# Group B's outputs summed by parts: the running product meets the steps of v

## The chip, the cores and the metric

The kernel runs on one core of a Trainium2 chip. The metric is the time of one execution on the device in microseconds (us), taken as the median of several runs. Matmuls and transposes run on TensorE (PE), elementwise work on VectorE (DVE), ScalarE (ACT) and GpSimd (POOL). The queue of SyncE (SP) issues most transfers (DMAs), which 16 DMA engines carry out. SBUF is the on-chip memory with 128 partitions, PSUM the one that matmuls write.

## The reference

One layer of a hybrid encoder over 1024 frames of width 1024: a normalisation, one projection to q, k and v, eight heads of chunked softmax attention (group A), eight heads of stick-breaking attention (group B), an output projection with a residual, and a gated channel mixer with a short convolution. The change concerns group B. Cut to what matters:

```python
for blk in range(S // Q_BLOCK):                 # 128 queries each
    z = einsum('bqhd,bkhd->bhqk', qb, kb) * scale
    causal = s_idx < t_idx                      # key strictly before query
    log_beta = log_sigmoid(z)
    log_1m = where(causal, log_beta - z, 0.0)   # log(1 - sigmoid(z))
    suffix = cumsum(log_1m, reverse=True) - log_1m
    a = where(causal, exp(log_beta + suffix), 0.0)
    outs.append(einsum('bhqk,bkhd->bqhd', a, vb))
```

The weight of a key is the sigmoid of its score times the product of (1 - sigmoid) over all keys between it and the query. With r(s) for the product of (1 - sigmoid) over the keys from s to the query, the weight of key s is r(s+1) - r(s).

## The kernel before

The program goes through stages: a start (the v projection, then q and k of the first head pair), group B, group A, the output projection, and the channel mixer. Keys and queries of group B are stored in reversed order of frames, so that the sum over earlier keys is a scan to the right. Two heads make a pair n (0 to 3); q, k and v of a pair fill 128 partitions or 128 columns.

**An item of group B** is one head h of one block i of 128 queries (class BlockB). ORDER_B runs the blocks 7, 0, 6, 1, 5, 2, 4, 3; block i has 8 - i key blocks, so its width is w = (8 - i) x 128 columns, 128 for block 7 and 1024 for block 0. PE computes the scores z into a PSUM tile (L803 and L804, names zb_i_h; the tiles come from a ring of two with the tag "big"), ACT makes them 1 - sigmoid (L812), DVE turns that into the running product by one scan (L813, into one of three acts tiles of 1025 columns, whose first column is 0), and a subtraction of neighbours over the full width gives the weights (L820). Two items later PE transposes the weights in blocks of 128 keys (L839, names tpb_i_h), ACT copies them to SBUF (L843, tb), and PE multiplies them with v to the outputs (L853, names yb). DVE copies these to y (L1214); once a pair is done they are split in two parts (yb again, L1153 and L1162) and stored to memory (spill, L1159).

**The filler.** Between these PE steps stand matmuls of the next pair's q and k projections (L145, into q_p and k_p), so that PE has work while an item waits for ACT and DVE. RATE_B says how many microseconds of them a group of 16 items gets. A projected half goes through DVE (L641, q_f and k_f), ACT and DVE again (L123), and POOL and a few transfers on SP bring its rows in place (L650, L663).

**The order of the work.** PE's order is written out. That of DVE, ACT, POOL and of SP's transfers is set by a planner (class Flow): chains of operations with estimated durations, of which always the one that can start first is emitted. Every engine runs its own list in order: an operation that waits holds up all behind it. The planner's clock goes by PE's estimated work and knows a transfer by a fixed rate and latency.

**v** was written to memory (v_d) by the v projection, 128 rows by (8 key blocks, 4 pairs, 128 columns) for each group. load_v(n) (L771) brings v of a pair to a tile v of 128 partitions (keys of a block) by 8 x 128, in one transfer, with four such buffers. Before group B it is called for n = 0 to 3, then for n + 4 after the last outputs of pair n. At the start q0 and k0 are projected in two halves of 512 frames, both halves in one PSUM tile of two banks.

Of the kernel before, what the change touches and what calls it, by code (L numbers as in the profile page):

```python
# [9 lines left out]
F32 = mybir.dt.float32  # L10
# [6 lines left out]
P = 128  # L17
# [3 lines left out]
G = 2  # L21
# [39 lines left out]
def tile_hybrid_block(  # L61
# [45 lines left out]
        return pool.tile(list(shape), dt, tag=tag, name=name)  # L107

    cst = one("cst", "cst", shape=(P, C_N))
    nc.scalar.dma_start(cst, consts)  # L110

    def c1(off):
        return cst[:, off : off + 1]
# [76 lines left out]
    with tc.tile_pool(name="kp", bufs=2) as kp:  # L190
# [280 lines left out]
        class Chain:  # L471


            def __init__(self, ops, t, after, behind, slack):
                self.ops, self.t, self.behind, self.slack = list(ops), t, behind, slack
                self.after = [a for a in after if a]
                self.begun = self.done = False

        class Flow:
# [14 lines left out]
            def start(self, c):  # L494
                if c.behind and not c.behind.begun or not all(a.done for a in c.after):
                    return None
                return max([c.t] + [self.free[e] for e in c.ops[0][0]] + [a.t for a in c.after])

            def step(self, limit=float("inf")):
                best = None  # L500
                for c in self.chains:
                    t = self.start(c)
                    if t is not None and t <= limit and (best is None or t < best[0]):
                        best = t, c
                if best is None:
                    return False
                t, c = best
# [38 lines left out]
        def on_s(n, do):  # L546
            return "S", n / 1200 + 0.1, 0.1, do
# [4 lines left out]
        def load(kb, do, us=2.2):  # L552
            return "D", kb / 260, us, do

        class Ring:
# [5 lines left out]
            def chain(self, *ops, after=(), then=(), slack=SLACK):  # L561

                head = flow.add(ops[0], after=[self.users[0], *after], behind=self.last)
                rest = flow.add(*ops[1:], after=[head, *then], slack=slack)
                self.users.popleft()
                self.users.append(rest)
                self.last = head
                return head, rest
# [40 lines left out]
        def fetch(queue=w_ready, pool=wp, tags=("wh", "wl"), bufs=None):  # L609

            if not w_next:
                return
            if (w_next[0] in LATE_W) != (queue is w_late):
                w_missed.append(1)
                return
            name, t, loaded = w_next
            w_next.clear()

            def high():
                t["h"] = pool.tile([P, D], F32R, tag=tags[0], name=f"{name}_h", bufs=bufs)  # L620
# [7 lines left out]
            c = flow.add(on_s(D, high), rest, after=[loaded], slack=SLACK)  # L628
            queue.append((t, c))
            load_next([c])  # L630

# [133 lines left out]

        def load_v(n):

            v_of[n] = kp.tile([P, T], F32, tag="v", name=f"v{n}", bufs=4)
            src = v_d[n // 4].rearrange("p (t n c) -> p t n c", n=4, c=P)[:, :, n % 4, :]
            v_chains[n] = [  # L770
                flow.add(load(512, lambda: nc.sync.dma_start(  # L771
                    v_of[n].rearrange("p (t c) -> p t c", c=P), src
                ), 4.0))
            ]

        HS = (A, B)

        class BlockB:

# [11 lines left out]
            def scores(self, h):  # L791
                i, nk = self.i, self.nk
                qa, qb, ka, kb, la, lb = qk_of[self.n]
                q, k, l = ((qa, ka, la), (qb, kb, lb))[h]
                z, mine = bigs.get(f"z{self.nm}_{h}")
                w = nk * P

                at, parts = {
                    1: (P, ((0, 2 * P, -P),)), 5: (192, ((192, 320, 0), (GW, 320, 320))),
                }.get(nk, (0, ((0, GW, 0), (GW, w - GW, GW)) if nk > 4 else ((0, w, 0),)))  # L800
                for o, n, k0 in parts:
                    ks = slice(i * P + k0, i * P + k0 + n)
                    PE.matmul(z[:, o : o + n], q[:, cols(i)], k[:, ks], start=True, stop=False)  # L803
                    PE.matmul(z[:, o : o + n], q[:, cols(i)], l[:, ks], start=False, stop=True)  # L804
# [6 lines left out]
                self.chain[h] = flow.add(  # L811
                    on_s(w + 75, lambda: S.activation(z, z, AF.Sigmoid, scale=-1.0)),  # L812
                    on_v(2 * w + 70, lambda: V.tensor_tensor_scan(  # L813
                        out=a[:, 1 : w + 1], data0=z, data1=first[:, :w], initial=1.0, op0=ALU.mult,
                        op1=ALU.max,
                    )),
                )
                mine.append(self.chain[h])
                self.chain[h] = flow.add(
                    on_v(w, lambda: V.tensor_tensor(  # L820
                        out=a[:, 1:w], in0=a[:, 1:w], in1=a[:, 2 : w + 1], op=ALU.subtract
                    ), "VL"),
                    after=[self.chain[h]],
                )
# [21 lines left out]
            def output(self, yy):  # L846
                ready(*self.turned)
                i, nk = self.i, self.nk
                v = v_of[self.n]
                for j in range(nk):  # L850
                    for h in range(2):
                        off = (i + j) * P + h * 64
                        PE.matmul(  # L853
                            yy[HS[h], :], v[:, off : off + 64],
                            self.at[h][:, self.c0[h] + j * P : self.c0[h] + (j + 1) * P],
                            start=j == 0, stop=j == nk - 1, skip_group_check=True,
                        )
                flow.work(0.218 * nk + 0.15)
# [209 lines left out]
        flow.free.update(V=START, S=START)  # L1068
        qk_chains[0] = []
        for what, stack in (("q", stack_q), ("k", stack_k)):  # L1070
            o = big(f"{what}0_p")
            outs = [o[:, rows(g)] for g in range(G)]
            st = stack(0, outs)
            w = pre["qk".index(what)]
            for g in range(G):
# [6 lines left out]
                qk_chains[0].append(next(st)[1])  # L1082
            fetch()
        S.preload_act_table_set("sigmoid_and_others")
        for n in range(4):
            load_v(n)
        flow.drain()
        start.__exit__(None, None, None)
# [82 lines left out]
            spilled[n] = flow.add(*ops, after=sum(parts, []) + spilled[n - 1 : n], slack=SLACK)  # L1171

        with stage("b"):
            b_acts = [pools["sbuf"].tile([P, T + 1], F32, tag=f"b{i}", name=f"acts{i}", bufs=1) for i in range(3)]
            for t in b_acts:
                GP.memset(t[:, :1], 0.0)
# [10 lines left out]
            for b in range(len(items) + 3):  # L1187
# [15 lines left out]
                if ending:  # L1203
# [82 lines left out]
        for b in range(len(blocks) + 2):  # L1286
# [13 lines left out]
            if b in (2, 3):  # L1300
                g = b - 2
                rn_chains["b", g] = flow_totals(yb_of[0][:, rows(g)], f"nb_{g}", rn2[:, 4 * g : 4 * g + 4])
                if g == 1:
                    rn_chains["b"] = flow_root(rn2, [rn_chains["b", g] for g in range(G)])
            if cur and cur.i == 2:
                if cur.p < 3:
                    load_bias(cur.p + 1)
# [779 lines left out]
def _layout(inputs):  # L2087
# [8 lines left out]
    def tiles(w):  # L2096
# [12 lines left out]
            cols(a("norm1_g")[0]), cols(a("norm2_g")[0]), cols(a("norm_a_g")[0]),  # L2109
            cols(a("norm_b_g")[0]), cols(a("final_g")), cols(conv_w[0]), cols(conv_w[1]),  # L2110
            cols(conv_w[2]), cols(a("conv_b")[0]), np.broadcast_to(rel[:, -1], (P, 8)),
        ],
        axis=1,
    )
# [32 lines left out]
```

## Time and profile before

| | us |
|---|---|
| median of 3 runs | 1218.7 (1218.18 to 1219.36) |
| the profiled execution | 1219.38 |
| its span in the trace | 1217.6 |
| PE busy in it | 1200.3 |
| DVE busy | 947.7 |
| ACT busy | 670.4 |
| POOL busy | 163.8 |

The span is what the hardware profiler saw between the first and the last instruction; the execution's own time has 1.8 us around it. An engine's busy time is the time in which it executes. Rows of groups give line, engine, operation, output and inputs, shape and count; then the busy time of all, the mean of one in ns, the idle time ahead of them, and what ended it. Rows of the timeline begin with start and duration in us; a bracket at their end gives the idle time ahead and its releaser. Group B runs from about 111 to 330 us, the start before it, group A after it.

### The profile page before, as it was taken

The numbers are of one execution on the slowest core, as the hardware profiler recorded it, in microseconds if no ns is written. First come the engines' busy times: TensorE is split into PE (matmuls) and PEld (weight loads), VectorE is DVE, ScalarE is ACT, GpSimd is POOL, SyncE is SP. The second block draws the span as 40 slices with busy tenths as digits, with TensorE's granted clock in tenths as the row PEclk, the third lists the DMA queues.
The fourth block names the chain that finished last, engine by engine and source line by source line (L and its number), as shares of the span: only waits on it lengthen the run. The fifth ranks groups of instructions, "written<-read, shape, count | busy, mean of one in ns | idle before, by whom it ended". The sixth has DMA issues, their size and how long they took to land.

```text
span 1217.6 us, 17209 instructions
## 1 busy us (share of the span) xinstructions
PE 1200.3 (99%) x6476; PEld 995.5 (82%) x6476; DVE 947.7 (78%) x1417; ACT 670.4 (55%) x1180; POOL 163.8 (13%) x128
## 2 busy tenths in 40 slices
PE   9999999999999999999999999999999999999997
PEld 6787888888878888888878888888888888888887
DVE  7945878889567677559997768777687779969896
ACT  7863454554576766434575555545555455444424
POOL 0002101212211112133000000000000023042036
PEclk9999999999999999999999999999999999999999
DMA  8354323433523382134032132221222196420003
GB/s 297 95 195 135 99 82 87 113 110 93 143 72 93 77 265 72 68 112 149 16 122 93 64 104 72 84 91 65 104 72 85 56 368 268 174 103 1 1 1 139
DMA packets 60323, 135.19 MB, mean 111 GB/s; under 512 B 6736, under 2 KB 18128, under 8 KB 60240
## 3 DMA queue, kind: packets, MB, share of 16 engines
q1 hardware_dynamic: 60096, 133.98, 33.7%
q8 instruction: 51, 0.84, 0.3%
q14 instruction: 32, 0.26, 0.1%
q10 hardware_dynamic: 144, 0.11, 0.1%
HBM read 89.24 MB, written 28.31 MB: 97 GB/s over the span
## 4 chain that ended last, share of the span: by engine, by line
PE 82%; DVE 7%; DMA 4%; ACT 3%; issue 2%; POOL 1%; SPq 0%; DVEq 0%; ACTq 0%; POOLq 0%
PE u_a L1563 9%; PE u_c L1563 9%; PE u_e L1563 8%; PE dz L2062 8%; PE q_p L145 6%; PE k_p L145 6%; PE u_b L1563 4%; PE dj L2062 4%; PE dm L2062 4%; PE v_x L454 3%; PE pa L145 3%; PE tpb L839 3%; PE yb L853 3%; PE v_y L454 2%; PE pb L145 2%
## 5 line engine op out<-in xcount | busy, mean ns | idle before, releaser
L813 DVE TENSOR_TENSOR_SCAN acts<-zb,first 128x128 f32<-128x128 f32 (+7 forms) x64 | 86.1, 1351 | 22.3 <-ACT zb L812 22.0
L843 ACT COPY tb<-tpb 128x128 f32<-128x128 f32 (+3 forms) x96 | 43.4, 483 | 62.3 <-PE tpb L839 61.6
L1587 DVE SCALAR_TENSOR_TENSOR vt<-cv,cst,vt 128x1023 f32<-128x1023 f32 (+1 forms) x44 | 58.2, 1322 | 2.2 <-ACT vt L1581 1.4
L1587 DVE SCALAR_TENSOR_TENSOR gt<-cg,cst,gt 128x1023 f32<-128x1023 f32 (+1 forms) x44 | 56.5, 1285 | 1.6 <-ACT gt L1581 0.8
L123 POOL TENSOR_TENSOR dx_0wl<-dr,dx_0wh 128x512 fp32r<-128x512 f32 x1 | 1.4, 1371 | 412.3 <-ACT dx_0wh L1829 412.3
L934 ACT ACTIVATE pa<-sa,sta 128x640 f32<-128x640 f32 (+4 forms) x64 | 42.3, 661 | 23.4 <-DVE sta L920 18.6
L812 ACT ACTIVATE zb<-zb 128x128 f32<-128x128 f32 (+7 forms) x64 | 41.2, 644 | 17.9 <-PE zb L804 17.1
L959 ACT COPY pta<-tpa 128x512 f32<-128x512 f32 (+3 forms) x80 | 37.2, 476 | 22.7 <-PE tpa L955 22.4
L145 PE MATMUL q_p<-hTh,q_h 128*128 128x512 f32 x112 | 47.4, 423 | 0.0
L820 DVE TENSOR_TENSOR acts<-acts 128x127 f32<-128x127 f32 (+7 forms) x64 | 46.8, 750 | 0.7
L1581 ACT ACTIVATE gt<-cg,cst 128x1024 f32<-128x1024 f32 x22 | 27.4, 1245 | 36.0 <-DVE cg L1455 35.9
L145 PE MATMUL k_p<-hTh,k_h 128*128 128x512 f32 x112 | 46.3, 413 | 0.4 <-DVE q_f L641 0.4
L145 PE MATMUL q_p<-hTh,q_l 128*128 128x512 f32 x112 | 44.1, 394 | 0.0
L145 PE MATMUL k_p<-hTl,k_h 128*128 128x512 f32 x112 | 44.0, 393 | 0.0
L123 POOL TENSOR_TENSOR q_l<-q_r,q_h 128x1024 fp32r<-128x1024 f32 x7 | 16.9, 2419 | 201.2 <-ACT q_h L621 146.8
L145 PE MATMUL k_p<-hTh,k_l 128*128 128x512 f32 x112 | 44.0, 393 | 0.0
L145 PE MATMUL q_p<-hTl,q_h 128*128 128x512 f32 x112 | 44.0, 392 | 0.0
L839 PE MATMUL tpb<-ident,acts 128*128 128x128 f32 x288 | 42.8, 276 | 0.2
L920 DVE TENSOR_REDUCE sta<-sa 128x1 f32<-128x640 f32 (+4 forms) x64 | 41.9, 655 | 1.3
L839 PEld LDWEIGHTS tpb<-ident,acts 128*128 128x128 f32 x288 | 33.8, 140 | 9.9 <-ACT tb L843 2.1
L1452 DVE TENSOR_TENSOR up_r<-up_r 128x512 f32<-128x512 f32 x60 | 41.2, 687 | 0.8
L955 PE MATMUL tpa<-ident,pa 128*128 128x128 f32 x240 | 38.7, 278 | 1.9 <-ACT pta L959 0.9
(1313 smaller groups left out, 3916.3 us busy)
## 6 DMA issues: line engine op xcount, KB each, us to landing
up_r<-in_w_up_dram SPq DMA_DIRECT2D x44, 512.0 KB, 3.6
act<-vt SPq DMA_DIRECT2D x22, 512.0 KB, 2.6
dr<-in_w_dn_dram SPq DMA_DIRECT2D x20, 512.0 KB, 6.8
dr<-act SPq DMA_DIRECT2D x20, 512.0 KB, 7.5
wv<-in_w_v_dram SPq DMA_DIRECT2D x16, 256.0 KB, 5.4
xin<-in_xT_dram SPq DMA_DIRECT2D x16, 256.0 KB, 5.4
row<-in_x_rows_dram SPq DMA_DIRECT2D x16, 256.0 KB, 2.6
v<-v_d SPq DMA_DIRECT2D x8, 512.0 KB, 5.3
```

What stands on the lines that cost most here:

```text
L145: PE.matmul(o, w[:, sl], t[:, rows(g)], start=first and i == 0, stop=last and i == 2,)
L454: PE.matmul(bank[j], t[:, cols(j)], w, start=p in (1, 5) and k == 0 and i == 0, stop=k == 3 and i == 2, skip_group_check=True,)
L812: on_s(w + 75, lambda: S.activation(z, z, AF.Sigmoid, scale=-1.0)),
L813: on_v(2 * w + 70, lambda: V.tensor_tensor_scan(out=a[:, 1 : w + 1], data0=z, data1=first[:, :w], initial=1.0, op0=ALU.mult, op1=ALU.max,)),
L820: on_v(w, lambda: V.tensor_tensor(out=a[:, 1:w], in0=a[:, 1:w], in1=a[:, 2 : w + 1], op=ALU.subtract), "VL"),
L839: PE.transpose(tp[:, cols(b)], self.a[h][:, cols(b0 + b)], ident)
L843: mine.append(flow.add(on_s(m * P, lambda o=o, tp=tp: S.copy(o, tp))))
L920: V.tensor_reduce(out=st[:, 0:1], in_=full, axis=AX.XY if nk == 5 else AX.X, op=ALU.max, negate=True,)
L934: on_s(w + 170, lambda: S.activation(po, full, AF.Exp, bias=st[:, 0:1], accum_out=st[:, 1:2])),
L1563: PE.matmul(o, w[:, cols(k)], t, start=start and k == 0 and i == 0, stop=k == 3 and i == 2, skip_group_check=True,)
L1587: V.scalar_tensor_tensor(out=t[:, : T - lag], in0=o[:, lag:], scalar=c1(c + ct), in1=t[:, : T - lag], op0=ALU.mult, op1=ALU.add,)
L2062: PE.matmul(o[m], w[:, cols(m)], t, start=i in (0, 1, 4, 5) and p == ps_[0] and j == 0, stop=p == ps_[-1] and j == 2, skip_group_check=True,)
```

## The change

The sum over keys of (r(s+1) - r(s)) v(s) is rearranged: it is the sum of r(s) times a step of v between neighbouring keys, with the ends kept apart. So the scan's result is transposed as it is, and a second array dv, v's neighbour minus v, takes the place of v in the outputs. For the first 128 keys of a block's list, which hold the diagonal, weights are still made, by a subtraction over 127 columns, and meet v.

The parts:

- the subtraction after the scan covers 127 columns for every item; the acts tiles have 1024 columns and need no memset;
- load_v brings for a pair of group B a tile dv and a tile v by four transfers (128 rows; 127 rows, shifted by one; the last row from the other blocks, 7 x 128; 128 zeros from widened constants), and DVE subtracts one from the other (128x1024, in place);
- with two tiles for each pair in the same four buffers, pairs 0 and 1 are loaded ahead of group B, pair 2 after pair 0, pair 3 after pair 1, pairs 4 and 5 after pair 2, pairs 6 and 7 in group A;
- the halves of q0 and k0 get PSUM tiles of their own, q's with the tag "big", k's with "pj";
- RATE_B is 19 for 20;
- the planner breaks ties: among chains that can start at the same time it takes the one that was ready first, with 1 us added for the weights' chains and those of the rings.

```diff
-RATE_B, LEAD_B = 20.0, 8.0
+RATE_B, LEAD_B = 19.0, 8.0
+DUE = 1.0
...
-                return max([c.t] + [self.free[e] for e in c.ops[0][0]] + [a.t for a in c.after])
+                ready = max([c.t] + [a.t for a in c.after])
+                return max([ready] + [self.free[e] for e in c.ops[0][0]]), ready + c.due
...
-            v_of[n] = kp.tile([P, T], F32, tag="v", name=f"v{n}", bufs=4)
             src = v_d[n // 4].rearrange("p (t n c) -> p t n c", n=4, c=P)[:, :, n % 4, :]
-            v_chains[n] = [
-                flow.add(load(512, lambda: nc.sync.dma_start(
-                    v_of[n].rearrange("p (t c) -> p t c", c=P), src
-                ), 4.0))
-            ]
...
+            d, o = whole(f"dv{n}")
+            v, nxt = whole(f"v{n}")
+            v_of[n] = v, d
+
+            def bring():
+                nc.sync.dma_start(o, src)
+                nc.sync.dma_start(nxt[: P - 1], src[1:])
+                nc.sync.dma_start(nxt[P - 1 :, : KT - 1, :], src[:1, 1:, :])
+                nc.sync.dma_start(nxt[P - 1 :, KT - 1, :], consts[:1, C_N:])
+
+            v_chains[n] = [flow.add(
+                load(1024, bring, 5.0),
+                on_v(T, lambda: V.tensor_tensor(out=d, in0=v, in1=d, op=ALU.subtract), "VL"),
+            )]
...
-                        out=a[:, 1 : w + 1], data0=z, data1=first[:, :w], initial=1.0, op0=ALU.mult,
+                        out=a[:, :w], data0=z, data1=first[:, :w], initial=1.0, op0=ALU.mult,
...
-                    on_v(w, lambda: V.tensor_tensor(
-                        out=a[:, 1:w], in0=a[:, 1:w], in1=a[:, 2 : w + 1], op=ALU.subtract
+                    on_v(P, lambda: V.tensor_tensor(
+                        out=a[:, : P - 1], in0=a[:, : P - 1], in1=a[:, 1:P], op=ALU.subtract
...
-                            yy[HS[h], :], v[:, off : off + 64],
+                            yy[HS[h], :], (d if j else v)[:, off : off + 64],
...
-            o = big(f"{what}0_p")
-            outs = [o[:, rows(g)] for g in range(G)]
+            outs = [(big if what == "q" else pj)(f"{what}0_p{g}")[:, :GW] for g in range(G)]
...
-        for n in range(4):
+        for n in range(2):
             load_v(n)
...
-                        load_v(n + 4)
+                        for m in ((2,), (3,), (4, 5), ())[n]:
+                            load_v(m)
```

In the two programs an instruction's line differs (L771 before is L791 to L794 after, L820 is L847, L813 is L840, L641 is L646, L123 is L124, L803 and L804 are L830 and L831, L839 is L866, L145 is L146). A number at a name's end only tells one tile from the next.

SP's list at the end of the start, before, from the last raw weights of pair 0 (k_r and q_r are raw weights of the next pair; v_949 to v_952 are v of pairs 0 to 3; qb and qa are pieces of the next pair's q):

```order
L605 DMA k_r<-in_w_in_dram 128x1024
L771 DMA v_949<-v_d_111 128x8x128
L771 DMA v_950<-v_d_111 128x8x128
L771 DMA v_951<-v_d_111 128x8x128
L605 DMA q_r<-in_w_in_dram 128x1024
L771 DMA v_952<-v_d_111 128x8x128
```

And after (dv_951 and v_952 belong to pair 0, dv_953 and v_954 to pair 1):

```order
L609 DMA k_r<-in_w_in_dram 128x1024
L791 DMA dv_951<-v_d_111 128x8x128
L792 DMA v_952<-v_d_111 127x8x128
L793 DMA v_952<-v_d_111 1x7x128
L794 DMA v_952<-in_consts_dram 1x128
L791 DMA dv_953<-v_d_111 128x8x128
L792 DMA v_954<-v_d_111 127x8x128
L793 DMA v_954<-v_d_111 1x7x128
L794 DMA v_954<-in_consts_dram 1x128
L609 DMA q_r<-in_w_in_dram 128x1024
```

Four transfers of 128 rows became two of 128 rows, two of 127 rows and four of one row, all behind the same k_r.

DVE's list at the start of group B, before, from the last operation on k0:

```order
L123 TENSOR_TENSOR lb_914<-k_f_955,kb_912 64x512
L641 SCALAR_TENSOR_TENSOR q_f_1045<-q_p_1008,rb_802 128x512
L123 TENSOR_TENSOR q_f_1045<-q_f_1045,qa_1033 128x512
L813 SCALAR_TENSOR_TENSOR acts_998<-zb_7_0_1052,first 128x128
L820 TENSOR_TENSOR acts_998<-acts_998 128x127
L641 SCALAR_TENSOR_TENSOR q_f_1076<-q_p_1035,rb_802 128x512
L813 SCALAR_TENSOR_TENSOR acts_999<-zb_0_0_1072,first 128x1024
```

And after:

```order
L124 TENSOR_TENSOR lb_916<-k_f_960,kb_914 64x512
L798 TENSOR_TENSOR dv_951<-v_952,dv_951 128x1024
L798 TENSOR_TENSOR dv_953<-v_954,dv_953 128x1024
L646 SCALAR_TENSOR_TENSOR q_f_1078<-q_p_1013,rb_802 128x512
L840 SCALAR_TENSOR_TENSOR acts_1006<-zb_7_0_1054,first 128x128
L646 SCALAR_TENSOR_TENSOR q_f_1087<-q_p_1040,rb_802 128x512
L840 SCALAR_TENSOR_TENSOR acts_1007<-zb_0_0_1070,first 128x1024
```

Both subtractions that make dv stand between the last operation on k0 and the first scan (a scan prints as SCALAR_TENSOR_TENSOR here, and as TENSOR_TENSOR_SCAN in the trace). On PE the scores of the third item, zb_0_1, follow those of the second directly in the changed order:

```order
L831 MATMUL zb_0_0_1070<-la_915,qa_843 128x512
L830 MATMUL zb_0_0_1070<-ka_913,qa_843 128x512
L831 MATMUL zb_0_0_1070<-la_915,qa_843 128x512
L830 MATMUL zb_0_1_1083<-kb_914,qb_844 128x512
L831 MATMUL zb_0_1_1083<-lb_916,qb_844 128x512
```

Before, 12 projection matmuls of k stood between them.

DVE's list where pair 1 begins and pair 2's v is brought, before (yb_1 is a part of pair 0's outputs, k_f a projected half of k):

```order
L813 SCALAR_TENSOR_TENSOR acts_998<-zb_1_0_1651,first 128x896
L1153 SCALAR_TENSOR_TENSOR yb_1_512_1696<-y_1051,cst,yb_0_512_1693 128x512
L641 SCALAR_TENSOR_TENSOR k_f_1701<-k_p_1532,rb_802 128x512
L820 TENSOR_TENSOR acts_998<-acts_998 128x895
L813 SCALAR_TENSOR_TENSOR acts_999<-zb_1_1_1661,first 128x896
```

And after:

```order
L840 SCALAR_TENSOR_TENSOR acts_1006<-zb_1_0_1633,first 128x896
L1179 SCALAR_TENSOR_TENSOR yb_1_512_1678<-y_1053,cst,yb_0_512_1599 128x512
L798 TENSOR_TENSOR dv_1556<-v_1557,dv_1556 128x1024
L646 SCALAR_TENSOR_TENSOR q_f_1685<-q_p_1472,rb_802 128x512
L840 SCALAR_TENSOR_TENSOR acts_1007<-zb_1_1_1646,first 128x896
L847 TENSOR_TENSOR acts_1006<-acts_1006 128x127
```

The subtraction for pair 2 stands ahead of the 127 columns of zb_1_0 (acts_1006). On PE, 36 projection matmuls stand between pair 0's last outputs and the first transposition of zb_1_0, where 45 stood; at the next change of pairs 30, where 39 stood; the subtraction for pair 3 stands there in the same way.

More of the change, by code (lines that the diff above doesn't have):

```diff
@@ L502, in step @@
                     t = self.start(c)
-                    if t is not None and t <= limit and (best is None or t < best[0]):
+                    if t is not None and t[0] <= limit and (best is None or t < best[0]):
                         best = t, c
@@ L564, in chain @@
                 rest = flow.add(*ops[1:], after=[head, *then], slack=slack)
+                head.due = rest.due = DUE
                 self.users.popleft()
@@ L628, in fetch @@
             c = flow.add(on_s(D, high), rest, after=[loaded], slack=SLACK)
+            c.due = DUE
             queue.append((t, c))
@@ L766, in load_v, with whole @@
         def load_v(n):
-            v_of[n] = kp.tile([P, T], F32, tag="v", name=f"v{n}", bufs=4)
             src = v_d[n // 4].rearrange("p (t n c) -> p t n c", n=4, c=P)[:, :, n % 4, :]
-            v_chains[n] = [
-                flow.add(load(512, lambda: nc.sync.dma_start(
-                    v_of[n].rearrange("p (t c) -> p t c", c=P), src
-                ), 4.0))
-            ]
+            def whole(name):
+                t = kp.tile([P, T], F32, tag="v", name=name, bufs=4)
+                return t, t.rearrange("p (t c) -> p t c", c=P)
+            if n >= 4:
+                v_of[n], o = whole(f"v{n}")
+                v_chains[n] = [flow.add(load(512, lambda: nc.sync.dma_start(o, src), 4.0))]
+                return
+            d, o = whole(f"dv{n}")
[10 more added lines that the diff above has]
+            )]
         HS = (A, B)
@@ L1173, in tile_hybrid_block @@
         with stage("b"):
-            b_acts = [pools["sbuf"].tile([P, T + 1], F32, tag=f"b{i}", name=f"acts{i}", bufs=1) for i in range(3)]
-            for t in b_acts:
-                GP.memset(t[:, :1], 0.0)
+            b_acts = [pools["sbuf"].tile([P, T], F32, tag=f"b{i}", name=f"acts{i}", bufs=1) for i in range(3)]
             first = pools["sbuf"].tile([P, T], BF16, tag="first", name="first", bufs=1)
```

10 lines of the change are left out of this document (7 added, 3 removed).

## The prediction

> **What bounds the kernel now.** First the busy times of the page, then the table by stage, because an average hides stages.
> ```profile
> PE 1200.3 (99%) x6476; PEld 995.5 (82%) x6476; DVE 947.7 (78%) x1417; ACT 670.4 (55%) x1180; POOL 163.8 (13%) x128
> ```
> ```profile
> core 0: us, PE busy (x) PEld busy (x) DVE busy (x) ACT busy (x) POOL busy (x), PEclk, DMA share, GB/s
> 86.00:130.00 44.00, 42.37 (x195) 34.42 (x194) 24.29 (x26) 20.16 (x31) 9.20 (x9) 1.00 0.53 160
> 130.00:180.00 50.00, 49.99 (x376) 42.01 (x374) 41.37 (x50) 25.37 (x49) 5.91 (x4) 1.00 0.32 85
> 180.00:230.00 50.00, 49.91 (x384) 41.61 (x384) 42.38 (x49) 27.90 (x53) 7.20 (x4) 1.00 0.40 110
> 230.00:280.00 50.00, 49.66 (x383) 41.55 (x379) 45.31 (x50) 27.42 (x52) 10.30 (x6) 1.00 0.40 107
> 280.00:335.00 55.00, 54.89 (x370) 46.43 (x369) 37.93 (x61) 28.17 (x52) 13.41 (x11) 1.00 0.42 113
> ```
> TensorE (PE) is busy for 1200.3 of 1217.6 us at the full granted clock. From 130 to 335 us, group B's stage, its idle time is 0.01 + 0.09 + 0.34 + 0.11 = 0.55 us. VectorE (DVE) works 41 to 45 us of each 50 there and PE never waits for it. So whatever the change saves on DVE can return at most 0.55 us; what it can cost is whatever makes PE wait. The execution took 1219.4 us, the span and 1.8 around it, and lies 0.7 above the median of the runs, 1218.7. I count from 1219.4.
>
> **The subtraction, cut to 127 columns.** It is the change's saving on DVE.
> ```profile
> L820 DVE TENSOR_TENSOR acts<-acts 128x127 f32<-128x127 f32 (+7 forms) x64 | 46.8, 750 | 0.7
> ```
> ```profile
> L820 DVE TENSOR_TENSOR acts<-acts 128x1023 f32<-128x1023 f32 x8 | 9.6, 1210 | 0.0
> L813 DVE TENSOR_TENSOR_SCAN acts<-zb,first 128x896 f32<-128x896 f32 x8 | 16.1, 2017 | 3.4 <-ACT zb L812 3.3
> L641 DVE SCALAR_TENSOR_TENSOR q_f<-q_p,rb 128x512 f32<-128x512 f32 x10 | 6.8, 679 | 3.0 <-PE q_p L145 2.9
> L813 DVE TENSOR_TENSOR_SCAN acts<-zb,first 128x128 f32<-128x128 f32 x8 | 3.3, 414 | 0.7 <-ACT zb L812 0.7
> L820 DVE TENSOR_TENSOR acts<-acts 128x127 f32<-128x127 f32 x8 | 2.3, 286 | 0.1
> ```
> 64 of them take 46.8 us; at 0.286 each 18.3 remain, and 28.5 go. The four new subtractions for dv (128x1024, the size of the 1.21 row) add 4.8. DVE loses 23.7 us, all of it beside PE's work: I take **-0.5** from the 0.55 of idle time.
>
> **PSUM tiles of q0 and k0.** The two long waits of window 86 to 130 are these.
> ```profile
> 94.58 0.39 PE L145 MATMUL q_p<-hTh,qk_l 128*128 128x512 f32 x1
> 95.81 0.50 PE L145 MATMUL q_p<-hTh,qk_h 128*128 128x512 f32 x1 [0.85 <-DVE q_f L641]
> ...
> 104.56 0.39 PE L145 MATMUL k_p<-hTh,qk_l 128*128 128x512 f32 x1
> 105.73 0.50 PE L145 MATMUL k_p<-hTh,qk_h 128*128 128x512 f32 x1 [0.78 <-DVE k_f L641]
> ```
> The second half's first matmul stands in the same PSUM tile as the first half and waits until DVE has read it. Starts lie 1.23 and 1.17 us apart where neighbours lie 0.23 apart. With a tile for each half both waits go: 1.00 + 0.94, **-1.9**. Next late is the weights' arrival, which no row shows late here.
>
> **The new load of v.** It decides the time. Before, v is one transfer of 128 rows for each pair; now a pair of group B needs two large ones and two small ones, and one large one has 127 rows (v shifted by a key). A subtraction on DVE waits for all four, and what stands behind it on DVE waits too.
> ```profile
> DMA packets 60323, 135.19 MB, mean 111 GB/s; under 512 B 6736, under 2 KB 18128, under 8 KB 60240
> ...
> v<-v_d SPq DMA_DIRECT2D x8, 512.0 KB, 5.3
> ```
> ```profile
> 102.20 0.33 SPq L605 DMA_DIRECT2D k_r<-in_w_in_dram  x1
> 102.64 3.64 SPq L771 DMA_DIRECT2D v<-v_d  x3
> ```
> ```profile
> DMA packets 2448, 1.24 MB, mean 309 GB/s; under 512 B 32, under 2 KB 2448, under 8 KB 2448
> ...
> q1 hardware_dynamic: 2448, 1.24, 112.2%
> ```
> The first row's 6736 packets under 512 B are 421 x 16, and the program issues 421 transfers: read as one closing packet from each engine, every transfer of before is cut into 16 equal shares (its row counts are 128 or 64). 127 is prime: no count from 2 to 16 divides it. So I bound the load from both sides. Spread over all engines it costs what the 512 KB row says, 5.3 us to landing. On one engine it moves 127 x 8 runs of 512 B = 520 KB at a sixteenth of the full queues' rate in the last fence (106 to 110 us), 309 / 16 = 19.3 GB/s: **27 us**. I take 27, since every transfer seen has equal shares and this one can have none.
>
> The Trainium skill, DMA: Bandwidth & Descriptors, section "Why a DMA increments its semaphore by 16 and not by 1", gives the count of engines as the largest number up to 16 that divides the slowest dimension on both sides, and names 127 partitions as a case of one engine; no run here shows such a transfer yet. By it the sum is the 1308.2 below; by an even spread it would be the 1218.0 of the first rival.
>
> *Start of group B.* In the changed order SP issues dv and v of pairs 0 and 1 behind k_r, from 102.6 us on. On the shared engine shares of 512 KB take 32.8 KB / 19.3 = 1.7 us: k_r 1.7, dv 1.7, v 27, dv 1.7, v 27, together 59; with about 2 us from issue to the first byte and landing, the last lands at 164.7. Both subtractions stand on DVE behind k0's last operation and ahead of this:
> ```profile
> 110.84 0.69 DVE L641 SCALAR_TENSOR_TENSOR k_f<-k_p,rb 128x512 f32<-128x512 f32 x1 [1.64 <-PE k_p L145]
> ...
> 116.16 0.68 DVE L123 TENSOR_TENSOR lb<-k_f,kb 64x512 fp32r<-64x512 f32 x1
> 116.87 0.69 DVE L641 SCALAR_TENSOR_TENSOR q_f<-q_p,rb 128x512 f32<-128x512 f32 x1
> ...
> 119.60 0.43 DVE L813 TENSOR_TENSOR_SCAN acts<-zb,first 128x128 f32<-128x128 f32 x1 [0.65 <-ACT zb L812]
> ```
> ```profile
> 118.80 0.28 PE L803 MATMUL zb<-ka,qa 128*128 128x256 f32 x1
> ...
> 122.46 0.39 PE L804 MATMUL zb<-la,qa 128*128 128x512 f32 x1
> 122.69 0.39 PE L145 MATMUL k_p<-hTh,k_h 128*128 128x512 f32 x1
> ```
> Last landing 164.7 + 1.2 + q_f 0.68 + scan 0.43 = 167.1, and only this scan frees the PSUM tile of zb_7_0. Two such tiles exist: zb_7_0 and zb_0_0 hold them, and zb_0_1, next on PE in the new order, needs the first. PE gets there at 122.69 - 1.9 = 120.7. **+46.4**.
>
> *Pairs 2 and 3.* v of pair 2 is asked for once pair 0's last outputs (36 matmuls from 170.98) are done, that of pair 3 once pair 1's are (from 217.41).
> ```profile
> 170.98 2.19 PE L853 MATMUL yb<-tb,v 128*64 128x128 f32 x36
> ...
> 190.59 0.27 PE L839 MATMUL tpb<-ident,acts 128*128 128x128 f32 x1
> ```
> ```profile
> 217.41 2.19 PE L853 MATMUL yb<-tb,v 128*64 128x128 f32 x36
> ...
> 235.73 0.49 PE L839 MATMUL tpb<-ident,acts 128*128 128x128 f32 x3
> ```
> Issue to landing is 0.8 + 1.7 + 27 + 2.2 = 31.7. On DVE the subtraction (1.2), q_f (0.68), a scan (2.02) and zb_1_0's 127 columns (0.29) follow before PE can transpose zb_1_0: 35.9. PE's work from the outputs' end, 172.9, to that transposition is 17.7 us with 45 projection matmuls; the lower RATE_B makes them come earlier, and in the new order 36 stand there: 9 x 0.23 less, so 15.7. **+20.2**. For pair 3 only the subtraction and one of 0.29 follow: 33.2, against 235.73 - 219.5 = 16.2 less 2.1 again (30 projection matmuls instead of 39), so 14.1. **+19.1**. Transfers queued behind these loads come later too, and PE has no more work to give them; a spill that a DVE step needs may add 3.
>
> *Restarts.* PE's first matmuls after it stood still:
> ```profile
> L212 PE MATMUL v_y<-zero x10: 379/622/634, 1.5 to 4.9; 128*128 128x512 bf16 x10
> ```
> Nine starts take 3.4 us, 0.38 each where 0.23 is normal: 1.5 us lost for ten. Three restarts: **+4.5** (0 to 6).
>
> The Trainium skill, TensorE: Matmul & The Clock Gate, Part 1, has PE at half rate after an idle window of about 3.4 us; its figure gives an estimate of 1.7 for each restart, and the L212 row agrees in kind.
>
> **RATE_B and DUE.** With projections moved earlier within each pair, those left between k of pair 3 and its first scores are 33, 33 x 0.23 = 7.5 us; from k_f at 110.84 to the first scores at 118.80 the chain took 8.0 in the trace. I take **+1** (0 to 2). The smaller memsets, the sliced constants and the new ties move nothing that PE waits for: 0.
>
> **Sum:** 1219.4 - 0.5 - 1.9 + 46.4 + 20.2 + 19.1 + 4.5 + 1 = **1308.2**.
>
> **The rivals.** *The load spreads.* If 127 rows go over many engines, the two pairs' dv and v are 2 x (0.524 + 0.520) = 2.09 MB; with k_r's 0.52 MB ahead, 2.61 MB at 309 GB/s from 102.6 us take 8.5, and with 2 us for issue and landing v of pair 1 is there at 113.1, ahead of DVE's last k0 step, which ends at 116.84 - 1.9 = 114.9 us. That landing is the point from which it decides: earlier, nothing waits and the sum is 1219.4 - 0.5 - 1.9 + 1 = 1218.0, not slower. For it speaks that the queues have room (a busy share of 0.32 to 0.42 in group B); against it, that equal shares can't be made. I give it 0.14.
> *One engine for each load, but not the same one.* Then the two first loads run side by side and end 28.7 us (v and dv) earlier: 1308.2 - 28.7 = 1279.5. No row here shows which engine a short transfer takes; 0.06.
> *A faster lone engine.* The page's busiest slice of 40 moved
> ```profile
> GB/s 297 95 195 135 99 82 87 113 110 93 143 72 93 77 265 72 68 112 149 16 122 93 64 104 72 84 91 65 104 72 85 56 368 268 174 103 1 1 1 139
> ```
> 368 GB/s, 23 for an engine: 22.6 us instead of 27, four times 4.4 less, 1308 - 17.6 = 1290. This lies inside the forecast.
>
> **How the numbers follow.** One engine 0.80 at 1308 (own range 1286 to 1328: the faster engine and no restarts below, 6 us of queued spills, restarts and three longer landings of 3 above), two engines 0.06 at 1279.5, spread 0.14 at 1218 (1216 to 1222). 8 in 10 need the first and most of the second: 1275 to 1328. A measurement of this kernel tells 0.2%, 2.4 us, from no change. Slower: 0.80 + 0.06 = 0.86; the spread case gives 0.08 to the same and 0.06 to faster.
>
> **What would show it.** Right: v's 127-row transfer takes 20 to 30 us to land, L798 waits for it on DVE, PE has one idle stretch of 40 to 50 us near 121 us and two of about 20, and q0/k0 show no wait at their second halves. Wrong: L798 starts within 2 us of the operation ahead of it, or a 127-row transfer lands like one of 128; then no term from 46.4 to 4.5 stands.

## The result and the profile after

| | us | against before, 95% interval |
|---|---|---|
| before, median of 4 runs | 1219.03 | |
| changed, median of 4 runs | 1291.95 (1290.78 to 1293.2) | 1.0597 (1.0584 to 1.0611) |
| its profiled execution | 1293.2 | |

The changed kernel is 6% slower, inside the predicted range and 16 us below the predicted 1308.2. The page's busy times and the chain that ended last:

```profile
PE 1204.9 (93%) x6476; PEld 1000.7 (77%) x6476; DVE 927.1 (72%) x1421; ACT 670.7 (52%) x1180; POOL 163.6 (13%) x125
...
PE 80%; SPq 8%; DVE 6%; ACT 2%; DMA 2%; issue 1%; POOL 1%; DVEq 0%; ACTq 0%; POOLq 0%
```

PE has the same 6476 matmuls; its share fell because the span grew. DVE lost 947.7 - 927.1 = 20.6 us, near the 23.7 worked out, and it bought nothing. New in the chain is SP's queue with 8%, where the page of before has 0%. The longest waits of PE, as engine, line, what it waited for, and total, times, longest in us:

```profile
PE zb L830 <- DVE acts L840: 38.3, 1, 38.3
PE tpb L866 <- DVE acts L847: 17.7, 2, 17.2
PE k_p L146 <- DVE q_f L646: 15.5, 1, 15.5
```

These are the three stretches that were forecast; with a short wait behind the second (0.6 us, in the second row) they make 71.5 us. By stage (the columns as before) they lie here:

```profile
86.00:130.00 44.00, 35.34 (x161) 28.90 (x159) 15.87 (x17) 17.24 (x26) 6.17 (x5) 0.93 0.31 104
130.00:180.00 50.00, 20.40 (x124) 16.90 (x124) 18.48 (x26) 10.10 (x19) 2.98 (x2) 0.65 0.27 73
180.00:230.00 50.00, 43.80 (x337) 36.49 (x335) 27.98 (x35) 22.39 (x42) 5.80 (x3) 0.96 0.20 53
230.00:280.00 50.00, 39.22 (x279) 32.36 (x280) 30.54 (x44) 19.92 (x39) 3.59 (x3) 0.87 0.35 96
280.00:335.00 55.00, 37.83 (x268) 31.95 (x266) 26.18 (x35) 19.43 (x37) 8.77 (x5) 0.84 0.28 76
```

From 130 to 180 us PE works 20.40 of 50 where it had 49.99, the granted clock falls to 0.65 with it, and DVE and ACT work 18.48 and 10.10 us where they had 41.37 and 25.37. SP's timeline (start, duration, issue) at the end of the start shows what stands behind them:

```profile
101.77 0.33 SPq L609 DMA_DIRECT2D k_r<-in_w_in_dram  x1
102.21 0.65 SPq L791 DMA_DIRECT2D dv<-v_d  x1
102.91 0.78 SPq L792 DMA_DIRECT2D v<-v_d  x1
103.74 23.95 SPq L793 DMA_DIRECT2D v<-v_d  x1
127.73 0.41 SPq L794 DMA_DIRECT2D v<-in_consts_dram  x1
128.26 0.57 SPq L791 DMA_DIRECT2D dv<-v_d  x1
128.94 0.68 SPq L792 DMA_DIRECT2D v<-v_d  x1
129.67 23.68 SPq L793 DMA_DIRECT2D v<-v_d  x1
```

L792 is the transfer of 127 rows. It is issued in 0.8 us, but the next instruction of SP, a transfer of 3.5 KB, takes 23.95 us to issue: SP is held. With pair 1's load it happens again (23.68 us). What was moved within this second hold, from 133 to 152 us:

```profile
DMA packets 807, 0.41 MB, mean 22 GB/s; under 512 B 0, under 2 KB 807, under 8 KB 807
...
q1 hardware_dynamic: 807, 0.41, 7.2%
```

Only 22 GB/s move, in packets of 512 B, at 7.2% of 16 engines where the full queues showed 112.2%: about a sixteenth of it. So one engine carries the 127 rows; 520 KB at 22 GB/s are 23.6 us, and SP is held as long. DVE in the same time:

```profile
131.64 1.23 DVE L798 TENSOR_TENSOR dv<-v,dv 128x1024 f32<-128x1024 f32 x1 [16.24 <-DMA v<-in_consts_dram]
157.38 1.22 DVE L798 TENSOR_TENSOR dv<-v,dv 128x1024 f32<-128x1024 f32 x1 [24.52 <-DMA v<-in_consts_dram]
158.53 0.68 DVE L646 SCALAR_TENSOR_TENSOR q_f<-q_p,rb 128x512 f32<-128x512 f32 x1
159.13 0.41 DVE L840 TENSOR_TENSOR_SCAN acts<-zb,first 128x128 f32<-128x128 f32 x1
```

The two subtractions wait for the last of the four transfers, and the first scan behind them starts at 159.13 where it stood at 119.60. ACT stands almost as long: the raw weights q_r, which SP issues behind both holds at 153.92, are converted at 158.07 after 35.69 us of idle time. Before, this conversion waited only for PE:

```profile
121.80 1.06 ACT L621 CAST q_h<-q_r 128x1024 fp32r<-128x1024 f32 x1 [2.30 <-PE q_p L145]
```

The two later stretches of PE read differently. On DVE, at pair 2's load:

```profile
236.72 0.75 DVE L1179 SCALAR_TENSOR_TENSOR yb<-y,cst,yb 128x512 fp32r<-128x512 f32 x1 [17.76 <-DMA spill<-yb]
237.39 1.22 DVE L798 TENSOR_TENSOR dv<-v,dv 128x1024 f32<-128x1024 f32 x1
```

and on ACT, at pair 3's:

```profile
303.19 0.72 ACT L1188 ACTIVATE yb<-y,cst 128x512 fp32r<-128x512 f32 x1 [18.67 <-DMA spill<-yb]
```

There the subtraction waits for nothing any more when its turn comes. What came last is a spill of 256 KB, which stands on SP behind the held L793 (held from 209.96 and 276.12 us, 22.9 and 23.2 us), and whose buffer a step of the outputs' split needs. PE's restart after its longest stretch:

```profile
159.59 0.79 PE L830 MATMUL zb<-kb,qb 128*128 128x512 f32 x1 [38.26 <-DVE acts L840]
160.19 0.63 PE L831 MATMUL zb<-lb,qb 128*128 128x512 f32 x1
160.61 0.63 PE L830 MATMUL zb<-kb,qb 128*128 128x512 f32 x1
...
164.45 0.63 PE L146 MATMUL k_p<-hTl,k_h 128*128 128x512 f32 x1
164.88 0.45 PE L146 MATMUL k_p<-hTh,k_l 128*128 128x512 f32 x1
```

Starts lie 0.43 us apart for 13 matmuls instead of 0.23: 2.6 us lost, and the granted clock is 0.50 from 155 to 165 us.

### The profile page after: what moved, and what is told of

Its sections match the earlier page's. It is cut to its first block, busy times and chain, and to the rows that moved or that the text cites. A ratio compares the mean times of both kernels' runs of the same rounds, so it can differ in the third digit from the quotient of the medians.

```text
span 1291.5 us, 17232 instructions
## 1 busy us (share of the span) xinstructions
PE 1204.9 (93%) x6476; PEld 1000.7 (77%) x6476; DVE 927.1 (72%) x1421; ACT 670.7 (52%) x1180; POOL 163.6 (13%) x125
## 4 chain that ended last, share of the span: by engine, by line
PE 80%; SPq 8%; DVE 6%; ACT 2%; DMA 2%; issue 1%; POOL 1%; DVEq 0%; ACTq 0%; POOLq 0%
PE u_c L1590 8%; PE u_e L1590 8%; PE u_a L1590 8%; PE dz L2089 7%; SPq L793 7%; PE k_p L146 5%; PE q_p L146 5%; PE u_b L1590 4%; PE dj L2089 4%; PE dm L2089 4%; PE pa L146 3%; PE pb L146 3%; PE v_x L455 2%; PE tpb L866 2%; PE v_y L455 2%; PE yb L880 2%
## 5 line engine op out<-in xcount | busy, mean ns | idle before, releaser
L840 DVE TENSOR_TENSOR_SCAN acts<-zb,first 128x128 f32<-128x128 f32 (+7 forms) x64 | 85.7, 1350 | 60.2 <-ACT zb L839 60.1
L146 PE MATMUL k_p<-hTh,k_h 128*128 128x512 f32 x112 | 47.9, 427 | 15.5 <-DVE q_f L646 15.5
L866 PE MATMUL tpb<-ident,acts 128*128 128x128 f32 x288 | 45.0, 286 | 17.7 <-DVE acts L847 17.7
L866 PEld LDWEIGHTS tpb<-ident,acts 128*128 128x128 f32 x288 | 36.1, 147 | 27.1 <-issue 18.6
L839 ACT ACTIVATE zb<-zb 128x128 f32<-128x128 f32 (+7 forms) x64 | 41.2, 643 | 29.6 <-PE zb L831 29.4
L830 PE MATMUL zb<-kb,qb 128*128 128x512 f32 (+3 forms) x48 | 19.5, 407 | 38.3 <-DVE acts L840 38.3
L124 POOL TENSOR_TENSOR dx_0wl<-dr,dx_0wh 128x512 fp32r<-128x512 f32 x1 | 1.4, 1368 | 412.4 <-ACT dx_0wh L1856 412.4
L146 PE MATMUL q_p<-hTh,q_h 128*128 128x512 f32 x112 | 46.2, 412 | 0.0
L124 POOL TENSOR_TENSOR q_l<-q_r,q_h 128x1024 fp32r<-128x1024 f32 x7 | 16.7, 2392 | 228.4 <-ACT q_h L625 181.2
L146 PE MATMUL k_p<-hTl,k_h 128*128 128x512 f32 x112 | 44.9, 401 | 0.0
L146 PE MATMUL k_p<-hTh,k_l 128*128 128x512 f32 x112 | 44.8, 400 | 0.0
L146 PE MATMUL q_p<-hTh,q_l 128*128 128x512 f32 x112 | 43.9, 392 | 0.0
L146 PE MATMUL q_p<-hTl,q_h 128*128 128x512 f32 x112 | 43.8, 391 | 0.0
L830 PEld LDWEIGHTS zb<-kb,qb 128*128 128x128 f32 x48 | 9.4, 196 | 39.7 <-DVE acts L840 38.7
```

What stands on the lines that cost most here:

```text
L146: PE.matmul(o, w[:, sl], t[:, rows(g)], start=first and i == 0, stop=last and i == 2,)
L840: on_v(2 * w + 70, lambda: V.tensor_tensor_scan(out=a[:, :w], data0=z, data1=first[:, :w], initial=1.0, op0=ALU.mult, op1=ALU.max,)),
L866: PE.transpose(tp[:, cols(b)], self.a[h][:, cols(b0 + b)], ident)
```

## The experiments

### The 127 rows cut in two

```diff
-                nc.sync.dma_start(nxt[: P - 1], src[1:])
+                nc.sync.dma_start(nxt[:112], src[1:113])
+                nc.sync.dma_start(nxt[112 : P - 1], src[113:])
```

> The changed kernel, with the 127-row transfer of v cut into 112 rows and 15 rows; nothing else is touched. Theory (127 rows have no equal share from 2 to 16, so they run on one engine, and SP, DVE and PE wait in turn): both pieces spread, land within 5 to 8 us, SP is not held, the subtractions for dv start without a wait of more than 2 us, the three idle stretches of PE (38.3, 15.6 and 17.3 us) are gone, and the time is 1216 to 1221 us. Rival 1 (SP is held by the small transfers of 7 x 128 and 1 x 128 themselves, 23.9 us each): they stay, and so does the time, 1285 to 1295. Rival 2 (the place of the subtractions ahead of the first scan costs PE, however soon v lands): at least 10 us of the first stretch stay, 1228 or more.

Measured: 1216.0 us, ratio 0.9978 (0.9969 to 0.9987). Both subtractions now start as soon as DVE is free:

```profile
113.97 0.68 DVE L124 TENSOR_TENSOR lb<-k_f,kb 64x512 fp32r<-64x512 f32 x1
114.69 2.36 DVE L799 TENSOR_TENSOR dv<-v,dv 128x1024 f32<-128x1024 f32 x2
116.97 0.68 DVE L646 SCALAR_TENSOR_TENSOR q_f<-q_p,rb 128x512 f32<-128x512 f32 x1
```

SP is not held; L793 is now the transfer of 15 rows:

```profile
102.18 0.65 SPq L792 DMA_DIRECT2D v<-v_d  x1
102.87 1.59 SPq L793 DMA_DIRECT2D v<-v_d  x1
```

The two small transfers are still there and take 0.7 and 0.4 us to issue: rival 1 falls. Of the first stretch 1.8 us are left in the list of waits, not 10, so rival 2 falls:

```profile
PE tpb L867 <- DVE acts L848: 1.8, 1, 1.8
```

One line of the load carries the whole loss. Between the two profiled executions it is 1293.2 - 1215.76 = 77.4 us.

### A middle dose

```diff
-                nc.sync.dma_start(nxt[: P - 1], src[1:])
+                nc.sync.dma_start(nxt[:122], src[1:123])
+                nc.sync.dma_start(nxt[122 : P - 1], src[123:])
```

> The changed kernel, with the 127-row transfer of v cut into 122 rows (2 x 61) and 5 rows: a middle dose. Theory (the number of engines is a number up to 16 that divides the rows): 122 rows run on two engines, 500 KB at 2 x 22 GB/s = 11.4 us each, SP is held about 11 us each time; the first idle stretch of PE is near 12 us (38.3 less twice 12.6), the other two near 4, and the time is 1235 to 1255. Rival (whatever is no multiple of 16 runs on one engine): about 23 us each, time 1280 to 1295. Rival (any cut frees it): 1216 to 1221.

Measured: 1244.6 us (one run), as the theory had it. Holds of SP (L793 is here the transfer of 5 rows) and PE's waits:

```profile
102.19 0.80 SPq L792 DMA_DIRECT2D v<-v_d  x1
103.04 11.59 SPq L793 DMA_DIRECT2D v<-v_d  x1
...
116.58 0.71 SPq L792 DMA_DIRECT2D v<-v_d  x1
117.34 11.43 SPq L793 DMA_DIRECT2D v<-v_d  x1
```

```profile
PE zb L831 <- DVE acts L841: 14.3, 1, 14.3
PE tpb L867 <- DVE acts L848: 5.8, 2, 5.2
PE k_p L146 <- DVE q_f L646: 3.8, 1, 3.8
```

The holds are 11.59 and 11.43 us, half of the 24; of the transfers from 118 to 126 us the last slices show 44 GB/s, twice the 22:

```profile
GB/s 205 297 335 348 307 228 182 141 90 56 36 23 33 38 26 28 18 23 44 44 44 44 44 44 44 44 44 44 44 44 44 44 44 44 44 44 44 44 44 44
```

So 122 rows, 2 x 61, ran on two engines. The pages of the profiles give a count as well. The prediction read the packets under 512 B as one closing packet from each engine that carries a transfer. With 127 rows, 122 + 5 and 112 + 15 the pages have:

```profile
DMA packets 64455, 137.29 MB, mean 106 GB/s; under 512 B 6772, under 2 KB 22260, under 8 KB 64372
DMA packets 64479, 137.29 MB, mean 110 GB/s; under 512 B 6796, under 2 KB 22284, under 8 KB 64396
DMA packets 64575, 137.29 MB, mean 113 GB/s; under 512 B 6892, under 2 KB 22380, under 8 KB 64492
```

The load of a pair of group B stands in the program four times. If the 127 rows have 1 engine, 2 + 5 in their place give 4 x 6 = 24 packets more, and 16 + 15 give 4 x 30 = 120 more: just what is there. Neither a multiple of 16 nor the mere cut decides, but into how many equal shares the rows go. The Trainium skill (DMA: Bandwidth & Descriptors, "Why a DMA increments its semaphore by 16 and not by 1") takes the largest number of engines up to 16 that divides the slowest dimension on both sides, here the rows. The runs with 127, 122 and 112 + 15 rows agree with it: 22 GB/s, 44 GB/s, and no hold.

### The subtraction out of the way

```diff
+        late = []
...
-            v_chains[n] = [flow.add(
-                load(1024, bring, 5.0),
-                on_v(T, lambda: V.tensor_tensor(out=d, in0=v, in1=d, op=ALU.subtract), "VL"),
-            )]
+            got = flow.add(load(1024, bring, (28.0, 52.0, 28.0, 28.0)[n]))
+
+            def steps():
+                v_chains[n] = [flow.add(
+                    on_v(T, lambda: V.tensor_tensor(out=d, in0=v, in1=d, op=ALU.subtract), "VL"),
+                    after=[got],
+                )]
+
+            if n < 2:
+                late.append(steps)
+            else:
+                steps()
...
         flow.drain()
+        for steps in late:
+            steps()
```

> The changed kernel with its 127-row transfers as they are, but the planner is told that v takes 28 us (52 for pair 1), so that the subtractions for dv stand later in DVE's list, behind the scans that do not need them. Theory (the first idle stretch comes from DVE waiting in order for v, the other two from transfers that SP, held by the full engine, issues too late): the first stretch shrinks from 38.3 to 20 us or less, what is left of it waits for transfers behind SP's hold, while the second and third keep 10 to 17 us each; time 1240 to 1265. Rival (all three come from the subtraction's place on DVE): all three go, 1218 to 1228. Rival (PE waits for v itself): nothing changes, 1285 to 1295.

Measured: 1296.7 us (one run), so the theory missed here, and the last rival's number is the nearest, for another reason: PE's list of waits has none for v. DVE runs the first scan at 117.29 and the second at 121.97, but PE's first stretch stays, 35.3 us in place of 38.3. ACT shows why:

```profile
120.93 1.01 ACT L849 ACTIVATE zb<-zb 128x1024 f32<-128x1024 f32 x1
158.09 1.04 ACT L625 CAST q_h<-q_r 128x1024 fp32r<-128x1024 f32 x1 [36.15 <-DMA q_r<-in_w_in_dram]
```

The next transfer in SP's list, the raw weights q_r, was issued at 153.17, after both holds. ACT's list has their conversion ahead of the next items' sigmoids, and so ACT stands for 36.15 us in place of DVE. The other two stretches stayed at 17.1 and 17.5, near the 10 to 17 of the theory. The common cause is thus not the place of the subtraction but SP's hold; which engine stands still depends on whose list meets a late transfer first.

### The transfer alone, in the kernel before

```diff
-                flow.add(load(512, lambda: nc.sync.dma_start(
-                    v_of[n].rearrange("p (t c) -> p t c", c=P), src
-                ), 4.0))
+                flow.add(load(512, bring, 4.0))
...
+            def bring():
+                if n < 2:
+                    nc.sync.dma_start(o[: P - 1], src[: P - 1])
+                    nc.sync.dma_start(o[P - 1 :], src[P - 1 :])
+                else:
+                    nc.sync.dma_start(o, src)
```

> The kernel before, but v of pairs 0 and 1 is brought as 127 rows and 1 row; no subtraction waits for them, and the outputs use v as before. Theory (a 127-row transfer runs on one engine, and the cost comes from what waits for it in order): SP is held about 24 us twice, from 103 to 153 us; v of pair 0 lands near 130, ahead of the first outputs at 136.7, and PE waits only for pair 1's q and k, whose moves stand behind SP's hold: 1219 to 1232. Rival (the slow transfer itself slows matmuls or other traffic): 1235 or more. Rival (127 rows alone are not slow, the four transfers together are): SP is held less than 5 us, 1218 to 1220.

Measured: 1254.2 us (one run): the holds are there (22.87 and 23.02 us), but the sum was out again, since it too left out the conversion of q_r in ACT's list. ACT waits 38.4 us for q_r, and PE has one stretch:

```profile
PE zb L810 <- DVE acts L820: 34.7, 1, 34.7
```

With no step of v, no subtraction and full weights, two transfers of 127 rows cost 35 us by themselves. The time lies in the range of the first rival, but its reason does not hold: from 106 to 125 us, while the slow transfer ran, PE was busy throughout with 85 matmuls, where it has 86 in the kernel before.

The last two runs halve the dose and then take SP out. Only pair 0's v comes as 127 + 1 rows:

```diff
-                if n < 2:
+                if n == 0:
```

> The kernel before, with only v of pair 0 brought as 127 rows and 1 row, on SP's queue as all the rest. Theory (SP is held until the one engine has nearly drained the transfer; what PE then lacks is behind SP, here the raw weights q_r for which ACT waits in order): one hold of 23 us, from 103.6 to 126.6; q_r lands near 135 instead of 158, PE's one idle stretch is 34.9 - 23.7 = 11 us, time 1228 to 1234. Rival (a fixed cost once any 127-row transfer is there): near 1254. Rival (v itself is waited for): v of pair 0 lands at 130, ahead of the first outputs at 136.7, so nothing is lost: 1218 to 1220.

Measured: 1233.9 us (one run); one hold of 23.08 us, q_r's conversion at 135.55, one stretch of PE and the restart behind it, as the theory had it:

```profile
PE zb L810 <- DVE acts L820: 12.4, 1, 12.4
```

The last run moves this one transfer to ACT's queue:

```diff
-                    nc.sync.dma_start(o[: P - 1], src[: P - 1])
+                    nc.scalar.dma_start(o[: P - 1], src[: P - 1])
```

> The same as before_v0_on_sp, but the 127-row transfer is issued from ACT's queue, the 1 row and everything else from SP's. Theory (it is SP's list that is held, and the transfers behind it on SP): SP is held nowhere over 3 us, the transfer still takes its 24 us on one engine, q_r lands before ACT needs it at 121.9, and PE loses nothing: 1218 to 1223. Rival (the engine itself is what others wait for, since every transfer has a share on it): q_r lands after 130 all the same and the time is 1226 to 1234.

Measured: 1225.2 us (one run), 2 us over the expected span, while the 21 runs of the kernel before beside it lie between 1218.1 and 1220.3. SP is held nowhere (q_r issued at 114.14), and ACT converts q_r at 121.78, in time. PE's new wait in group B is for v itself:

```profile
PE yb L860 <- DMA v<-v_d: 2.9, 1, 2.9
```

The transfer was issued at 105.8 and awaited until 139.7, 34 us where its bytes alone take one engine 23.6. In this time SP's queue moved 2.40 MB. If a sixteenth of that, 0.15 MB, went over the same engine at 22 GB/s, it took 6.8 of the 10 us, an estimate; the engine's share was not measured apart. When group A starts, this kernel is 4.4 us behind the kernel before (the first scores of A at 324.2 and 319.8): the 2.9 of this wait and the slow matmuls after it (granted clock 0.81 from 136 to 145 us). Another 1.1 us come in the channel mixer, where one wait of PE for ACT takes 1.4 and not 0.3; why is open. So the 12.4 us of wait belong to the held queue, and with another queue the slow transfer costs only its own lateness.

### Where the rest of the change stands

> The kernel before with one edit of the change: the halves of q0 and k0 have PSUM tiles of their own. Theory (two waits of 0.85 and 0.78 us and their pipeline gaps go): 1.9 us faster, 1216.5 to 1217.5, both waits gone from the list. Rival (what is late next gives it back in group B, since DVE and the transfers there do not come earlier): within 0.7 us of before, 1218.2 to 1219.2.

```diff
-            o = big(f"{what}0_p")
-            outs = [o[:, rows(g)] for g in range(G)]
+            outs = [(big if what == "q" else pj)(f"{what}0_p{g}")[:, :GW] for g in range(G)]
```

Measured: 1216.48 us beside 1218.95 of before, ratio 0.9979 (0.9971 to 0.9988), with both waits gone from the list. The same edit the other way round, in rows_112_15:

> rows_112_15 with the PSUM edit undone: both halves of q0 and of k0 in one tile again, everything else of the change kept. Theory (the split of these tiles is the whole gain of the mended change; cut subtractions and steps of v bring PE nothing, since DVE was not waited for): 1218.0 to 1219.2, the two waits of 0.8 us are back. Rival (23.7 us less on DVE are worth something by themselves): 1216.5 to 1217.8.

Measured: 1219.04 us, ratio 0.9997 (0.9988 to 1.0006), with the two waits of 0.8 us back. So the split of PSUM tiles is the whole gain of the change, as far as intervals of 1 us either way can tell: with it and nothing else 0.9979, with the mended rest 0.9978, with the rest alone 0.9997.

Two attempts to gain more from the mended kernel gave nothing. The first gives the mended load the late subtractions of subtract_later, with other times told to the planner:

```diff
-            got = flow.add(load(1024, bring, (28.0, 52.0, 28.0, 28.0)[n]))
+            got = flow.add(load(1024, bring, 5.0 + (6.0, 24.0, 0.0, 0.0)[n]))
```

> rows_112_15 with the subtractions for dv of pairs 0 and 1 added to the planner's list only after the start, so that they stand on DVE behind the first scans and not ahead of them. Theory (the 2.4 us of two subtractions ahead of the first scan cost PE its one long wait there, 1.98 us at 123 us): that wait goes, 1213.5 to 1215.3. Rival (the wait is only moved to the next item, since the subtractions cost DVE the same further on): 1215.5 to 1216.5.

Measured: 1215.85 us, ratio 0.9977 (0.9968 to 0.9986): the wait of 1.8 us is gone, the total is not lower, as the rival had it. Waits for ka and la at pair 2's first scores, 0.4 each in rows_112_15, are 1.4 and 0.2 us here. The second sets RATE_B back in that kernel:

```diff
-RATE_B, LEAD_B = 19.0, 8.0
+RATE_B, LEAD_B = 20.0, 8.0
```

> rows_112_15_later with RATE_B at 20 again. Theory (with 19 fewer projections stand between the items of a pair, more are left for the pair's end, and the next pair's first scores wait for transfers of k, 1.4 and 0.2 us at 206 us): these waits shrink to under 0.3 us and the time is 1213.8 to 1215.2. Rival (the pacing only moves the waits to other places): 1215.4 to 1216.4.

Measured: 1217.75 us, ratio 0.9991 (0.9982 to 1.0), slower than either expected. The waits at pair 2's first scores went, one of 0.9 us for la came at pair 3's, and in group A PE waits longer:

```profile
PE tpa L993 <- DVE pa L966: 1.3, 2, 1.0
PE tpa L993 <- DVE sa L954: 1.2, 1, 1.2
```

Why group A suffers from a rate in group B was not tried.

## Why the prediction held, step by step

**What bounds the kernel**: right. 20.6 us less on DVE brought nothing that shows (0.9997 for the rest alone). The saving was put at 23.7 because a subtraction over 127 columns was taken at 0.286 us; in rows_112_15 the 64 of them take 21.0 us, 0.34 each.

**PSUM tiles, -1.9**: right, and a little more when alone: 1218.95 - 1216.48 = 2.5 us.

**The load on one engine**: right, and shown from both sides, by 127, 122 and 112 + 15 rows in the changed kernel and by 127 rows in the kernel before. Its size was too high: I took the rate of an engine from a stretch in which all 16 were full, 19.3 GB/s; alone it moved 22, and a load of a pair (dv and v) took 25.7 us (131.64 to 157.38) instead of 28.7. The rival of a faster lone engine had 23 GB/s and 1290, the nearest number of all.

**Start of group B, +46.4**: 38.3, just under the 40 to 50 that was named as a sign of being right. The scan ran at 159.1 to 159.5 instead of 166.7 to 167.1, which is 7.6 of the 8.1 between: the last load was there for DVE at 157.4, not 164.7. (The sum is also written unclearly: 102.6 + 59 and 2 us give 163.6; the 164.7 takes the 3.0 us, 0.8 + 2.2, of the sum for pairs 2 and 3.) The mechanism as written, DVE held in order by the subtractions, is what the profile shows last; but it was not necessary. The prediction overlooked that SP itself would be held, and that ACT's list has q_r's conversion in the same place: ACT stood until 158.07, DVE until 157.38, and with DVE set free the stretch was still 35.3 us.

**Pairs 2 and 3, +20.2 and +19.1**: 15.5 + 0.6 and 17.2. Size nearly right, the last step wrong: not the subtraction but spills behind SP's hold came last. The prediction had them only as up to 3 us more. That its sums come out near is luck: v itself was hardly earlier than the spill. DVE began 3.9 us after L794 was issued at pair 0 (127.73 to 131.64). The same from 232.91 at pair 2 gives 236.8, an estimate, where the spill let DVE go at 236.7.

**Restarts, +4.5**: too low. The first cost 2.6; the granted clock is at 0.50 for about 4 to 5 us after each of the three, which makes some 7 in all, an estimate from the spacing of the first. The Trainium skill (TensorE: Matmul & The Clock Gate, Part 1) has PE back at the full rate after at least one busy window of about 3.4 us. Here the first restart took 5.3 us (159.59 to 164.88), which is more than one such window.

**RATE_B, +1**: about right in size (waits of 0.5 us for ka and 0.5 for la), but they came at pair 2's first scores, not pair 3's. The prediction's words were also wrong: a lower rate puts fewer projections between items and leaves more for the end of a pair. With the late subtractions, 19 gave 0.9977 and 20 gave 0.9991, and their intervals touch; in rows_112_15 itself 20 was not tried.

**The sum**: against the mended kernel's profile 77.4 us. The stretches are 71.5, less the 1.8 that the mended one has left, plus 7 of restarts, the estimate above: 76.7. The terms of the prediction for the same are 90.2; of the 13.5 us between, the start of group B has 8. So the measured time lies inside the range with one term too high by 8, two too high by 4 and 2, and one too low by 2.5.

## What to carry to other kernels

Look at the row count of each transfer before its bytes: 127 rows in one transfer held the queue for 24 us, where 112 and 15 held it for less than 2. A slow transfer must be read on its queue first: what stands behind it there, in whoever's list, is late, and moving the visible waiter out of the way only shows the next one. And before an edit lightens an engine, ask who waits for that engine: here PE's idle time in group B, 0.55 us, bounded the gain.

## What the runs showed of the hardware

A transfer on one engine was issued quickly (0.8 us), but the next issue on SP's queue was held until it had nearly drained (in the changed kernel 22 GB/s went on for some 1.8 us after the first hold ended at 127.7), 23 to 24 us for 1016 runs of 512 B on one engine and 11.5 for 976 on two. In all these runs the next issue was a transfer of 1 or 5 rows; one of 128 rows directly behind was not tried. From ACT's queue the same transfer did not hold SP, and it was there after 34 us; ACT issued no later transfer, so whether ACT's queue would have been held is not shown. A lone engine moved 22 GB/s in such runs, more than the 19.3 for each engine in a full stretch.
